# Nine conditioning steps spread through the first half's second merge, and residual tiles for the last recurrent block in the second half alone

## The chip, the cores and the metric

One core of a Trainium2 chip runs the kernel. The metric is the device time of one execution in microseconds; several executions are timed and their median stands. TensorE is called PE here, VectorE DVE, ScalarE ACT, GpSimd POOL and SyncE SP.

## The reference

One decoder layer for a prompt of 1024 tokens and for 8 samples of 4 tokens, which share the weights. Model width is 1024.

```python
mod = silu(c) @ ada_w + ada_b                       # conditioning: 6 x 1024 values per sequence
sh1, sc1, gt1, sh2, sc2, gt2 = split(mod, 6)
h = rmsnorm(x, norm1_g) * (1 + sc1) + sh1
u_x, u_g, u_q, u_k, u_v, u_r, u_lr, u_ga, u_gb = split(h @ w_in)
xc = causal_conv(u_x)
y_a = rg_lru(xc) * gelu(u_g)                        # 10 recurrent blocks of 128 channels
y_b = norm(gla_chunked(u_q, u_k, u_v, u_lr)) * silu(u_r)
m = sigmoid(u_ga) * (y_a @ proj_a) + sigmoid(u_gb) * (y_b @ proj_b)
x = x + gt1 * (m @ w_out)
h2 = rmsnorm(x, norm2_g) * (1 + sc2) + sh2
f1, f2 = split(h2 @ ffn_w1)
x = x + gt2 * ((silu(f1) * f2) @ ffn_w2)
```

The outputs are the two activations and the states of the convolution, of the recurrence and of the chunked branch.

## The kernel before

The tokens are worked in two halves: A has 512 columns of the prompt, B the other 512 and the 32 of the samples. Activations stand with channels in partitions. A weight is loaded in f32 (tiles `raw`, a ring of 5), and split into a high and a low part of a narrower type (tiles `hl`, a ring of 3; ACT writes the high part at line 154, DVE the low one at 155). A product then takes three matrix multiplications per 128 input channels: high by high, high by low and low by high (lines 452, 453, 454).

**The merge.** For each of eight blocks j of 128 output channels, a first loop makes the gate `gbpsa` (24 matrix multiplications) and the product `pbpsa` with `proj_b` (24, from eight tiles `yba`), and keeps their combination `mba` (line 1207). That loop is woven with the recurrent blocks. Then a second loop, `merge_a`, makes for each j the gate `gapsa` (24) and the product `papsa` with `proj_a`: 15 matrix multiplications with the weight tile `pa0` and the recurrent outputs `yaa0` to `yaa4`, and 15 with `pa1` and `yaa5` to `yaa9`.

**The conditioning steps.** `ada_w` is 48 quarters of 512 KB, named ada00 to ada113 (chunk 0 to 11, quarter 0 to 3). The last eight chunks belong to the generator `ada_rest`: each step multiplies one quarter (line 212) and loads the next one, only one ahead; it puts the load into a buffer of the S ring (17 buffers, shared with many activations), from SP's queue at line 203. After four quarters a chunk is turned: ACT copies it (line 217), PE transposes it four times (line 223), DVE puts it into `mod` (225, 226, 260). `s.ada(n)` takes n steps. Other generators of half A (`values`, `qk`, `r_tiles`, `merge_b`) take most of them, and nine are left behind the first merge loop: they are the last quarter and the turn of chunk 10, the four quarters and the turn of chunk 11, and two empty steps.

**What else runs there.** `weight_sums` loads pairs of weight tiles `s1`, `s2` (named `s_raw` in the profile) into the same ring of `raw` tiles, makes sums of them on DVE (lines 352 to 355) and has POOL write them out (357 when 353 is done, 356 when 355 is done). `paced_sums` has POOL copy one column of a gate's tile into a `sums` tile (line 387), so that the load behind it (388) doesn't start earlier than that gate; DVE sums them (392 to 396), and POOL writes (398). A scheduler of the framework orders each engine's instructions by priority and readiness as it estimates them, and `AHEAD` lifts the weights' splits. So an edit in one place can change the order on several engines.

**The recurrent block.** `lru_gate` makes the decay `a` and the state `hh` of a block. Both are in one tile of the S ring, except for the last block, where two tiles of the X ring (8 buffers, which also hold the residuals) are taken: lines 1100 to 1104. The exponential of line 1106 writes `a`; DVE then makes the input (1109, 1122), scans (1129), multiplies with the gelu gate (1138), and the result is split (188, 189) into `yaa`.

Of the kernel before, what the change touches and what calls it, by code (L numbers as in the profile page):

```python
# [18 lines left out]
NR = 10  # L19
# [35 lines left out]
def hybrid_layer(ctx, tc, I, O):  # L55
# [32 lines left out]
    def S(name, dt=F32):  # L88
        return sbig.tile([P, 2 * 544], dt, tag="S", name=name)

    def T(name, w=544):
        return tp.tile([P, w], F32, tag="t", name=name)
# [50 lines left out]
    def load_raw(src, n, name):  # L143
        raw = wp.tile([P, 1024], F32, tag="raw", name=name + "_raw", bufs=5)
        sp.dma_start(raw[:, :n], src)
        return raw
# [169 lines left out]
    def drain(g):  # L316
        for _ in g:
            pass

    def chain(*gs):  # L320
        for g in gs:
            yield from g

    def weave(g, extra, n):
        for w in g:
            yield w + sum(next(extra, 0.0) for _ in range(n))

    def side(g, extra):
        for w in g:
            next(extra, None)  # L330
            yield w
        yield from extra

    def mix(main, fill):
        credit = 0.0
        for want in main:
            credit = min(credit, 3.0) - want
            while credit < 0:
                got = next(fill, None)
                if got is None:  # L340
                    break
                credit += got
# [60 lines left out]
    class Half:  # L403
# [684 lines left out]
        def lru_gate(s, nb, m, xc):  # L1088
            N, n = s.N, f"{s.n}{nb}"
            gw = load_raw(I["lru_w"][nb], 256, "lw" + n)  # L1090
            g1, g2 = s.wide("g1" + n), s.wide("g2" + n)
            for g, c in (g1, 0), (g2, P):
                for o, w, bank, off in [(0, HP, 0, 0)] if s.hf == 0 else s.parts:
                    pe.matmul(g[:, bank, off:off + w], gw[:, c:c + P], xc[:, o:o + w], start=True, stop=True)
            tr, ti = T("tr" + n), T("ti" + n)
            for t, g, b in (tr, g1, nb), (ti, g2, 10 + nb):
                for o, p in s.over(t, g):
                    act.activation(o, p, AF.Tanh, scale=0.5, bias=vh[:, b:b + 1])
            dve.scalar_tensor_tensor(ti[:, :N], ti[:, :N], 1.0, xc[:, :N], op0=OP.add, op1=OP.mult)
            if nb < NR - 1:  # L1100
                both = S("la" + n)
                a, hh = both[:, :N], both[:, 544:544 + N]
            else:
                a, hh = [xp.tile([P, 544], F32, tag="X", name=k + n)[:, :N] for k in ("la", "lh")]
            s4 = sp4[:, nb:nb + 1]
            act.activation(a[:, :N], tr[:, :N], AF.Exp, scale=s4, bias=s4)
            act.activation(tr[:, :N], tr[:, :N], AF.Tanh, scale=s4, bias=s4)
            act.activation(m, a[:, :N], AF.Square)
            dve.scalar_tensor_tensor(m, m, 1.0, tr[:, :N], op0=OP.add, op1=OP.mult)
            return a, hh, ti  # L1110
# [160 lines left out]
        def merge_a(s):  # L1271
            s.m = []
            for j in range(KD):
                tg = s.gate_a(j)
                s.join(j, tg, s.over(tg, s.branch_a(j)))
                s.keep_m(j)
                next(sums_late, None)
                if j % 3 < 2 and j < 7:
                    next(sums_of, None)
# [372 lines left out]
        def branches(s, before):  # L1652
            s.y_a, s.os_ = [None] * NR, []
            b0, b1, v0, v1 = [], [], [], []
            head = chain(s.lr(), s.qk(0, b0))
            if before is not None:
                mix(before, head)
            drain(head)
            g0, g1 = s.values(0, v0), weave(s.values(1, v1), s.adas, 1)
            f = weave(s.qk(1, b1), s.adas, 1)  # L1660
            r = weave(s.r_tiles(), s.adas, 2)
            l = s.lru()
            fill = chain(g0, f, g1, r, l)
            mix(s.gla(0, *b0, g0, v0), fill)
            drain(f)
            mix(side(s.gla(1, *b1, g1, v1), s.head_norm(0)), fill)
            mix(chain(iter([6]), s.head_norm(1)), fill)
            drain(r)
            s.y_b_tiles()
            for w in s.merge_b():  # L1670
                next(l, None)
                next(l, None)
                s.ada(1)
            drain(l)
            drain(s.adas)
            if s.hf:
                pool.dma_start(O["tails"], tails)
            s.merge_a_fast() if s.hf else s.merge_a()
            s.back()
# [137 lines left out]
```

## Time and profile before

| | |
|---|---|
| median of 3 runs | 1961.77 us (1960.86 to 1966.2) |
| profiled execution | 1960.34 us, span 1958.6 us |
| mean granted clock of PE | 0.997 |
| PE busy | 1926.0 us, 13380 matrix multiplications |
| PE's waits on conditioning loads | 6.0 us in 2 waits |

The page gives busy times per engine and the waits with the instruction that ended them. In a timeline, a row has the start and duration in us, the engine and the line, and the tiles written and read; "x8" is a run of eight equal instructions, and a bracket is idle time ahead of the row and what released it. Matrix multiplications overlap, so their pitch is taken from the starts. The sum on the execution starts from 1960.34 us.

### The profile page before, as it was taken

The page shows a single profiled execution, that of the slowest core. Times are in us where ns is not written, and L with a number is a line of the kernel's source. Part 1 is how long each engine was busy: PE and PEld are TensorE (multiplying, and loading weights), DVE is VectorE, ACT ScalarE, POOL GpSimd, SP SyncE. Part 2 cuts the span into 40 slices and gives each one's busy share as a digit, 9 for nine tenths or more (in the row PEclk, how much of TensorE's full clock was granted, in tenths as well). Part 3 has the DMA queues.
Part 4 walks back from the last instruction along what each step waited for, and adds up shares of the span by engine and source line. Part 5 has one row for each costly group of instructions (what it writes and reads, how often), then busy time and mean ns, then how long its engine had stood idle before and what let it go on. Part 6 is the DMA issues. An engine that isn't in the chain of part 4 may idle for free. (4 is left out here: it accounts for less than half of the span.)

```text
span 1958.6 us, 33971 instructions
## 1 busy us (share of the span) xinstructions
PE 1926.0 (98%) x13380; PEld 1753.1 (90%) x13380; DVE 1360.2 (69%) x2420; ACT 973.2 (50%) x1559; POOL 140.7 (7%) x279
## 2 busy tenths in 40 slices
PE   9999999998999999999999999999999999999997
PEld 5877877776899998999899998999999999999997
DVE  5638487774658774677664497786467688888867
ACT  4645375542235552555353366675244354656653
POOL 0000001121100000000000001041201000000000
PEclk9999999999999999999999999999999999999999
DMA  8324235578764357554332413334446534555553
GB/s 341 108 97 165 73 108 193 195 264 315 260 235 157 128 179 247 189 183 156 119 119 68 145 49 96 128 115 148 145 140 226 199 130 131 177 170 179 178 163 104
DMA packets 122240, 319.24 MB, mean 163 GB/s; under 512 B 14560, under 2 KB 29664, under 8 KB 122080
## 3 DMA queue, kind: packets, MB, share of 16 engines
q1 hardware_dynamic: 107536, 263.89, 40.9%
q0 software_dynamic: 14000, 52.62, 7.4%
q8 instruction: 105, 1.72, 0.4%
q10 hardware_dynamic: 544, 0.56, 0.1%
q14 instruction: 55, 0.45, 0.1%
HBM read 278.42 MB, written 38.59 MB: 162 GB/s over the span
## 5 line engine op out<-in xcount | busy, mean ns | idle before, releaser
L155 DVE TENSOR_TENSOR fwa_hl<-fwa,fwa_hl 128x1024 fp32r<-128x1024 f32 (+1 forms) x57 | 68.8, 1207 | 44.6 <-ACT fwa_hl L154 43.6
L155 DVE TENSOR_TENSOR fwb_hl<-fwb,fwb_hl 128x1024 fp32r<-128x1024 f32 (+1 forms) x64 | 77.2, 1207 | 27.7 <-ACT fwb_hl L154 27.7
L154 ACT ACTIVATE fwa_hl<-fwa 128x1024 fp32r<-128x1024 f32 (+1 forms) x57 | 59.3, 1040 | 44.0 <-PE fapsa L1431 10.8
L154 ACT ACTIVATE fwb_hl<-fwb 128x1024 fp32r<-128x1024 f32 (+1 forms) x64 | 66.6, 1041 | 23.4 <-PE fcpsb L1431 9.0
L452 PE MATMUL f3psa<-faa,f3a_hl 128*128 128x512 f32 x176 | 68.6, 390 | 0.6 <-ACT f3a_hl L154 0.6
L454 PE MATMUL f3psa<-faa,f3a_hl 128*128 128x512 f32 x176 | 68.5, 390 | 0.4 <-DVE f3a_hl L155 0.4
L453 PE MATMUL f3psa<-faa,f3a_hl 128*128 128x512 f32 x176 | 68.6, 390 | 0.0
L154 ACT ACTIVATE f3a_hl<-f3a_raw 128x768 fp32r<-128x768 f32 (+1 forms) x32 | 25.4, 792 | 55.7 <-PE f3psa L454 47.4
L155 DVE TENSOR_TENSOR f3a_hl<-f3a_raw,f3a_hl 128x768 fp32r<-128x768 f32 (+1 forms) x32 | 28.3, 888 | 17.4 <-ACT f3a_hl L154 17.0
L452 PEld LDWEIGHTS f3psa<-faa,f3a_hl 128*128 128x128 f32 x176 | 33.0, 188 | 7.7 <-ACT f3a_hl L154 1.0
L454 PEld LDWEIGHTS f3psa<-faa,f3a_hl 128*128 128x128 f32 x176 | 33.0, 188 | 7.6 <-DVE f3a_hl L155 0.9
L453 PEld LDWEIGHTS f3psa<-faa,f3a_hl 128*128 128x128 f32 x176 | 33.0, 188 | 6.8
L352 DVE TENSOR_TENSOR s_raw<-s_raw 128x512 f32<-128x512 f32 x16 | 11.1, 691 | 37.9 <-DMA s_raw<-in_ffn 37.8
L454 PE MATMUL wopsb<-mb,wob_hl 128*128 128x272 f32 x128 | 36.9, 288 | 0.0
L452 PE MATMUL wopsb<-mb,wob_hl 128*128 128x272 f32 x128 | 36.9, 289 | 0.0
L453 PE MATMUL wopsb<-mb,wob_hl 128*128 128x272 f32 x128 | 36.8, 288 | 0.0
L453 PE MATMUL wopsa<-ma,woa_hl 128*128 128x256 f32 x128 | 36.4, 284 | 0.0
L454 PE MATMUL wopsa<-ma,woa_hl 128*128 128x256 f32 x128 | 36.2, 283 | 0.0
L452 PE MATMUL wopsa<-ma,woa_hl 128*128 128x256 f32 x128 | 36.1, 284 | 0.0
L212 PE MATMUL adaps<-ada,cth 128*32 128x256 f32 x384 | 29.5, 397 | 6.2 <-DMA ada<-in_ada_w 6.0
L452 PE MATMUL uxpsa<-h1a,uxpsa_hl 128*128 128x512 f32 x80 | 32.3, 403 | 0.0
L155 DVE TENSOR_TENSOR fvb_hl<-fvb,fvb_hl 128x768 fp32r<-128x768 f32 x28 | 26.8, 956 | 7.7 <-ACT fvb_hl L154 7.4
(2404 smaller groups left out, 7944.9 us busy)
## 6 DMA issues: line engine op xcount, KB each, us to landing
ada<-in_ada_w SPq DMA_DIRECT2D x48, 512.0 KB, 7.9
fwb<-wsum SPq DMA_DIRECT2D x72, 256.0 KB, 3.4
s_raw<-in_ffn SPq DMA_DIRECT2D x32, 512.0 KB, 4.3
wsum<-s_raw POOLq DMA_DIRECT2D x32, 512.0 KB, 4.2
fwa<-wsum SPq DMA_DIRECT2D x64, 256.0 KB, 3.3
fwb<-in_ffn SPq DMA_DIRECT2D x54, 256.0 KB, 3.4
fwa<-in_ffn SPq DMA_DIRECT2D x48, 256.0 KB, 3.1
woa_raw<-in_w_out SPq DMA_DIRECT2D x13, 512.0 KB, 4.2
```

The source lines that it names most:

```text
L154: act.activation(hl[:, 0, :n], raw[:, :n], AF.Copy)
L155: dve.tensor_sub(hl[:, 1, :n], raw[:, :n], hl[:, 0, :n].bitcast(F32))
L212: pe.matmul(ps[32 * g:32 * g + 32, c:c + 256], cth[:, 4 * (k % 2) + g, :], raw[:, g * 256:(g + 1) * 256], start=(k % 2 == 0), stop=(k % 2 ...
L352: dve.tensor_add(r2[:, 512:1024], r2[:, 0:512], r2[:, 512:1024])
L452: pe.matmul(out, wh, x[:, o:o + w], start=st, stop=False)
L453: pe.matmul(out, wh, x[:, N + o:N + o + w], start=False, stop=False)
L454: pe.matmul(out, wl, x[:, o:o + w], start=False, stop=en)
```

## The change

In `merge_a` of half A, each of the eight blocks now takes two conditioning steps, one between gate and product and one behind the product's combination. The `drain(s.adas)` between the two merge loops is gone. The last recurrent block's `a` and `hh` come from an S tile in half A, as for the other blocks, and from two X tiles in half B only.

```diff
@@ -1097,7 +1097,7 @@
-            if nb < NR - 1:
+            if s.hf == 0 or nb < NR - 1:
                 both = S("la" + n)
                 a, hh = both[:, :N], both[:, 544:544 + N]
             else:
@@ -1272,8 +1272,10 @@
             for j in range(KD):
                 tg = s.gate_a(j)
+                s.ada(1)
                 s.join(j, tg, s.over(tg, s.branch_a(j)))
                 s.keep_m(j)
+                s.ada(1)
                 next(sums_late, None)
@@ -1672,7 +1674,6 @@
                 s.ada(1)
             drain(l)
-            drain(s.adas)
             if s.hf:
                 pool.dma_start(O["tails"], tails)
             s.merge_a_fast() if s.hf else s.merge_a()
```

On every engine the order changes between the end of the first merge loop and the second loop of half A; ahead of and behind that it is the same.

**SP's queue** at the loads for the second merge loop. The numbers behind a name are tile numbers; `gapsa`, `pa0`, `pa1` are weights of the merge, `s1`, `s2` the pairs for the sums, `ada` the quarters. Before, ada100 stands ahead of these rows:

```order
L145 DMA pa1a0_raw_3794<-in_proj_a 128x640
L145 DMA s113_raw_3825<-in_ffn1 128x1024
L145 DMA s213_raw_3827<-in_ffn1 128x1024
L145 DMA gapsa1_raw_3836<-in_w_in 128x1024
L203 DMA ada101_3566<-in_ada_w 128x1024
L203 DMA ada102_3626<-in_ada_w 128x1024
L203 DMA ada103_3686<-in_ada_w 128x1024
L203 DMA ada110_3692<-in_ada_w 128x1024
L203 DMA ada111_3709<-in_ada_w 128x1024
L203 DMA ada112_3715<-in_ada_w 128x1024
L203 DMA ada113_3721<-in_ada_w 128x1024
L145 DMA pa0a1_raw_3868<-in_proj_a 128x640
```

And now:

```order
L145 DMA pa1a0_raw_3750<-in_proj_a 128x640
L145 DMA s113_raw_3781<-in_ffn1 128x1024
L145 DMA s213_raw_3783<-in_ffn1 128x1024
L145 DMA gapsa1_raw_3792<-in_w_in 128x1024
L203 DMA ada100_3344<-in_ada_w 128x1024
L145 DMA pa0a1_raw_3834<-in_proj_a 128x640
L145 DMA pa1a1_raw_3854<-in_proj_a 128x640
L145 DMA s114_raw_3892<-in_ffn1 128x1024
L203 DMA ada101_3565<-in_ada_w 128x1024
L203 DMA ada102_3625<-in_ada_w 128x1024
L203 DMA ada103_3685<-in_ada_w 128x1024
L203 DMA ada110_3723<-in_ada_w 128x1024
```

ada100 has moved behind `gapsa1` (it stood three rows ahead of `pa1a0`), ada101 to ada110 behind s114, which waits for POOL's write of s113. ada111 and ada112 come after s115 and s215, and ada113 after s116 and s216.

**DVE** from the sums of s113 to the first product's last tiles. Before, the recurrent blocks 8 and 9 stand well ahead of s113, just before the sums of the pair s111 and s211:

```order
L1109 SCALAR_TENSOR_TENSOR lma8_3310<-lma8_3310,tra8_3317 128x512
L396 TENSOR_TENSOR sums10_3468<-sums10_3468 128x256
L1109 SCALAR_TENSOR_TENSOR lma8_3310<-lma8_3310,tra9_3333 128x512
L1122 TENSOR_TENSOR tia8_3318<-tia8_3318,lma8_3310 128x512
L1122 TENSOR_TENSOR tia9_3334<-tia9_3334,lma8_3310 128x512
L1129 SCALAR_TENSOR_TENSOR laa8_3322<-laa8_3322,tia8_3318 128x512
L352 TENSOR_TENSOR s211_raw_3606<-s211_raw_3606 128x512
```

And now, behind the sums of s113:

```order
L355 TENSOR_TENSOR s113_raw_3781<-s113_raw_3781 128x512
L1207 SCALAR_TENSOR_TENSOR mba6_3601<-gba6_3380,pbpsa6_3571 128x512
L155 TENSOR_TENSOR pa0a0_hl_3732<-pa0a0_raw_3730,pa0a0_hl_3732 128x640
L1109 SCALAR_TENSOR_TENSOR lma8_3310<-lma8_3310,tra9_3333 128x512
L392 TENSOR_TENSOR sums31_3674<-sums31_3674 128x256
L1207 SCALAR_TENSOR_TENSOR mba7_3661<-gba7_3562,pbpsa7_3631 128x512
L1122 TENSOR_TENSOR tia8_3318<-tia8_3318,lma8_3310 128x512
L1122 TENSOR_TENSOR tia9_3334<-tia9_3334,lma8_3310 128x512
L1129 SCALAR_TENSOR_TENSOR laa8_3322<-laa8_3322,tia8_3318 128x512
L1129 SCALAR_TENSOR_TENSOR laa9_3338<-laa9_3338,tia9_3334 128x512
L1138 SCALAR_TENSOR_TENSOR gga8_3412<-laa8_3322,gga8_3412 128x256 x2
L1138 SCALAR_TENSOR_TENSOR gga9_3509<-laa9_3338,gga9_3509 128x256 x2
```

The recurrences of both blocks now stand behind L392 of `sums31` and `mba7`, and ahead of the split of `pa1a0` and of `yaa8`, `yaa9`, which come next. One exponential of line 1106 also has a new wait: for the buffer of `yba0`, which is free when block 7's third matrix multiplication is done.

**PE** at the end of the first merge loop. Before:

```order
L452 MATMUL pbpsa7_3632<-yba7_2243,pba7_hl_3635 128x512
L212 MATMUL adaps10_3565<-ada101_3566,cth_141 32x256 x4
L453 MATMUL pbpsa7_3632<-yba7_2243,pba7_hl_3635 128x512
L454 MATMUL pbpsa7_3632<-yba7_2243,pba7_hl_3635 128x512
L452 MATMUL gapsa0_3741<-h1a0_333,gapsa0_hl_3744 128x512
L453 MATMUL gapsa0_3741<-h1a0_333,gapsa0_hl_3744 128x512
L212 MATMUL adaps10_3565<-ada102_3626,cth_141 32x256 x4
```

And in the first product of `merge_a` now (ada100 stands where ada101 stood above):

```order
L453 MATMUL papsa0_3729<-yaa3_2586,pa0a0_hl_3732 128x512
L212 MATMUL adaps10_3564<-ada101_3565,cth_141 32x256 x4
L454 MATMUL papsa0_3729<-yaa3_2586,pa0a0_hl_3732 128x512
L452 MATMUL papsa0_3729<-yaa4_2790,pa0a0_hl_3732 128x512
L453 MATMUL papsa0_3729<-yaa4_2790,pa0a0_hl_3732 128x512
L454 MATMUL papsa0_3729<-yaa4_2790,pa0a0_hl_3732 128x512
L452 MATMUL papsa0_3729<-yaa5_2916,pa1a0_hl_3752 128x512
L212 MATMUL adaps10_3564<-ada102_3625,cth_141 32x256 x4
```

ada100 has moved from the end of gate 7 (ahead of block 6's product) to there; ada103 comes behind `yaa6`, ada110 ahead of `gapsa2`, ada111 behind the third matrix multiplication of `papsa2`, ada112 ahead of `gapsa3`, ada113 behind the third of `papsa3`.

## Prediction

> **What bounds the kernel now.** I read the page's head first, then the waits of PE, then PE's timeline and the windows around the longest wait, and last the queues that feed it.
>
> ```profile
> span 1958.6 us, 33971 instructions
> PE 1926.0 (98%) x13380; PEld 1753.1 (90%) x13380; DVE 1360.2 (69%) x2420; ACT 973.2 (50%) x1559; POOL 140.7 (7%) x279
> PE adaps L212 <- DMA ada<-in_ada_w: 6.0, 2, 5.6
> ```
>
> PE is busy for 98% of the span: it is the bound, and any time it stands still or runs slowly is on the path. Its largest wait (total, times, longest) is for a load of conditioning weights, 5.6 us at one place. That place is where the change works. PE's timeline there (start, us, instruction, and idle time ahead of it in brackets):
>
> ```profile
> 431.31 0.60 PE L223 MATMUL adat<-ident,accadar 128*128 128x128 f32 x4
> 431.66 0.48 PE L452 MATMUL gbpsa<-h1a,gbpsa_hl 128*128 128x512 f32 x1
> ...
> 436.99 0.39 PE L454 MATMUL gbpsa<-h1a,gbpsa_hl 128*128 128x512 f32 x1
> 437.39 0.64 PE L212 MATMUL adaps<-ada,cth 128*32 128x256 f32 x8
> ...
> 442.87 0.39 PE L452 MATMUL pbpsa<-yba,pba_hl 128*128 128x512 f32 x1
> ...
> 448.31 0.39 PE L452 MATMUL pbpsa<-yba,pba_hl 128*128 128x512 f32 x1
> 454.28 1.08 PE L212 MATMUL adaps<-ada,cth 128*32 128x256 f32 x8 [5.58 <-DMA ada<-in_ada_w]
> ...
> 459.49 0.39 PE L452 MATMUL gapsa<-h1a,gapsa_hl 128*128 128x512 f32 x1
> 459.81 0.64 PE L212 MATMUL adaps<-ada,cth 128*32 128x256 f32 x8
> 460.71 0.39 PE L454 MATMUL gapsa<-h1a,gapsa_hl 128*128 128x512 f32 x1
> ...
> 475.22 0.39 PE L452 MATMUL gapsa<-h1a,gapsa_hl 128*128 128x512 f32 x1
> ```
>
> The two rows at 442.87 and 448.31 are the 22nd matrix multiplication of the merge's blocks 6 and 7, 24 apart: 5.44/24 = 0.227 us each at full clock. From 459.49 to 460.71 lie one conditioning step and two of these (the second stands between the rows shown): 1.22 - 0.45 = 0.77 us for the step. The transposes cost 431.66 - 431.31 = 0.35. From 448.54 (448.31 + 0.227) to 475.22 PE does 56 matrix multiplications (2 of block 7, 24 of the gate, 30 of the product), 7 conditioning steps and 2 transposes: 12.7 + 5.4 + 0.7 = 18.8 us of work. It takes 26.7, so **7.8 us are lost**: 5.58 as the wait, some 2.2 behind it. The windows tell what the 2.2 are (columns: us; busy us of PE, PEld, DVE, ACT, POOL; PE's granted clock, DMA share, GB/s):
>
> ```profile
> 436.00:448.00 12.00, 11.99 (x59) 9.30 (x58) 6.80 (x13) 3.96 (x6) 3.43 (x7) 1.00 0.91 286
> 454.00:459.00 5.00, 4.72 (x22) 2.20 (x23) 4.96 (x10) 0.74 (x1) 1.99 (x4) 0.53 1.02 411
> ```
>
> The granted clock is 0.53 for the five us behind the wait. So the step behind the wait takes 1.08 us, the same step at 459.81 takes 0.64. Another wait of PE, of 2.37 us, leaves no such trace: the matmuls behind it take 0.70 and 0.62.
>
> ```profile
> 1180.13 0.70 PE L1094 MATMUL g1b1l<-xcb,lwb_raw 128*128 128x272 f32 x2 [2.37 <-issue]
> 1180.66 0.62 PE L1094 MATMUL g1b1r<-xcb,lwb_raw 128*128 128x272 f32 x2
> ```
>
> [...]
>
> **Why the load is late** is seen on SP's queue (start, issue time).
>
> ```profile
> 429.02 0.33 SPq L203 DMA_DIRECT2D ada<-in_ada_w  x1
> 444.27 1.24 SPq L145 DMA_DIRECT2D s_raw<-in_ffn  x2
> 446.03 9.72 SPq L203 DMA_DIRECT2D ada<-in_ada_w  x7
> ```
>
> The seven loads are issued together from 446.03, behind two loads for the weight sums; PE wanted the first at 448.5.
>
> **The change part by part.** It adds and removes no arithmetic: the eight loads, eight steps and two turns are the same ones, later. So the sum is the 7.8 given back less the waits in the new places. The residual tiles cost nothing by themselves: no wait in this stretch is for an X tile. Their effect, with that of the order, is that the last recurrent block's la/lh takes a tile of the S ring that the merge's y_b tiles fill, so its exponential waits for block 7's third matrix multiplication, and DVE does that recurrence later. The first product's last tiles need it; I count it in (2).
>
> (1) The step that stood at 437.39 (load ada100) now stands behind 46 matrix multiplications: 437.22 + 46 x 0.227 = 447.7. Its load takes the buffer that block 7's 6th matrix multiplication frees, 437.22 + 30 x 0.227 + 0.4 = 444.4. A load's time to landing is bounded by these answers on DMA issues (KB each, median us; the first has minimum, median, maximum of all 48):
>
> ```profile
> DMA to landing us min/median/max: 3.5/7.9/13.6
> ada<-in_ada_w SPq DMA_DIRECT2D x1, 512.0 KB, 8.2
> s_raw<-in_ffn SPq DMA_DIRECT2D x2, 512.0 KB, 6.3
> s_raw<-in_ffn SPq DMA_DIRECT2D x2, 512.0 KB, 3.2
> ```
>
> At 8.2 the wait is 4.9; at 3.5, 0.2. I take 4.5, near the short end since only the first product's loads share the queue: **1.2 us**.
>
> (2) Next is ada101, in the middle of the first product. PE arrives at 448.9 + 0.77 + 37 x 0.227 = 458.1. The load stands on SP behind s114, which needs the buffer of s113, which is written out by POOL after four DVE operations; PE's progress has no part in it. So everything counts from T, the landing of s113 and s213:
>
> ```profile
> 424.65 0.68 DVE L354 TENSOR_TENSOR s_raw<-s_raw 128x512 f32<-128x512 f32 x1
> 427.58 0.68 DVE L355 TENSOR_TENSOR s_raw<-s_raw 128x512 f32<-128x512 f32 x1
> 451.73 0.69 DVE L352 TENSOR_TENSOR s_raw<-s_raw 128x512 f32<-128x512 f32 x1 [6.89 <-DMA s_raw<-in_ffn]
> 454.34 0.68 DVE L355 TENSOR_TENSOR s_raw<-s_raw 128x512 f32<-128x512 f32 x1
> wsum<-s_raw POOLq DMA_DIRECT2D x2, 512.0 KB, 8.0
> wsum<-s_raw POOLq DMA_DIRECT2D x2, 512.0 KB, 3.8
> ```
>
> Before, T is 451.7. In the new order L355 of an earlier pair (s111) follows L354 at once, 427.58 - 425.25 = 2.3 earlier, and the 512 KB of ada100 are no longer ahead (0.52 MB at 286 GB/s = 1.8): the pair is issued at 444.27 - 4.1 = 440.2. With 6.3 to land, **T = 446.5** (443.4 with 3.2; 451.7 if nothing moves). Then four DVE operations (454.34 - 451.73), the write, s114's issue and ada101's: T + 2.6 + 5.3 + 0.8 + 5.5 = 460.7, with the write between 3.8 and 8.0 and the load between 3.5 and 8.2. **Wait 2.6** (0 to 13.2). Close to the 2.37 case, so I let the clock stand.
>
> DVE has a chain of its own: POOL's second `sums` load waits through gate 7 for the merge's block 6, and DVE's L392 on it stands ahead of the recurrence and the product's split.
>
> ```profile
> 440.10 1.45 POOL L388 DMA_DIRECT2D sums<-in_ffn  x2 [0.18 <-POOL sums L387]
> sums<-in_ffn POOLq DMA_DIRECT2D x2, 256.0 KB, 5.7
> 416.28 1.30 DVE L1122 TENSOR_TENSOR tia<-tia,lma 128x512 f32<-128x512 f32 x2 [2.16 <-ACT lma L1155]
> 417.49 1.22 DVE L1129 TENSOR_TENSOR_SCAN laa<-laa,tia 128x512 f32<-128x512 f32 x1
> 428.19 0.75 DVE L1138 SCALAR_TENSOR_TENSOR gga<-laa,gga 128x256 f32<-128x256 f32 x2
> 454.94 0.68 DVE L1207 SCALAR_TENSOR_TENSOR mba<-gba,pbpsa 128x512 f32<-128x512 f32 x1
> 458.14 0.82 DVE L155 TENSOR_TENSOR pa1a_hl<-pa1a_raw,pa1a_hl 128x640 fp32r<-128x640 f32 x1
> ```
>
> That load goes out at T + 4.9 (2.6 as above, 0.6 for mba, 0.6 for ACT's tanh, 1.1 for POOL), lands 5.1 later (a little under 5.7), and DVE then needs 0.35 (half of an L352) + 0.6 + 1.25 + 2 x 1.2 + 2 x 0.75 + 0.75 = 6.8: T + 16.8 = 463.3. PE, held by ada101, reaches that split's low half at 460.7 + 2 steps + 6 matrix multiplications = 463.6. Nothing more is lost; if the load came early, this chain would still cost 463.3 - 461.0 = 2.3, so a fast load alone would change (2) little.
>
> (3) ada111 and ada113 go out behind loads that the split of a product's second tile releases, about 2.3 us after that product's end; PE needs them 24 + 3 matrix multiplications and a step later, 6.9. That leaves 4.6; at 5.4 to landing (between 3.2 and 6.3) **0.8 each**, 0 to 3.6 (at 8.2).
>
> Sum: 1.2 + 2.6 + 1.6 = 5.4 against 7.8: 2.4 us gained, 1960.34 - 2.4 = 1957.9 on the profiled execution's basis. The median shown, 1961.77, is 1.4 above that execution, so 1959.4 is my figure.
>
> [...]
>
> **The rivals.** *All is hidden.* Loads land in 3.5 and T is 443.4: ada101 lands by 458, DVE's chain ends before PE comes at 461.0, the waits come to about 1, and 6.8 are gained: 1955.0. Against it: T needs every step early, and the DMA engines' share is 0.91 to 1.02 in the windows shown. Chance 0.12.
>
> *Transfers stay as slow as before* (the side that is slower). T stays 451.7, the write takes 8.0, loads 8.2. ada100 waits 4.9, the clock falls (2.2), PE arrives at 458.1 + 3.7 + 2.2 = 464.0; ada101 lands at 451.7 + 2.6 + 8.0 + 0.8 + 8.2 = 471.3: 7.3 and again 2.2; with (3) 18.2, a loss of 10.4: 1972.2. It decides from where waits and slow clock pass 7.8. For it: the median landing of 7.9. Against: the burst of seven loads is gone. Chance 0.12.
>
> *The later pair is the stall.* ada111 and ada113 at 8.2 wait 3.6 each, and the clock falls twice: 1.2 + 2.6 + 2 x (3.6 + 2.2) = 15.4, a loss of 7.6: 1969.4. Against: no burst of seven loads is in those stretches, and the pair of `s_raw` loads lands in 3.2 to 6.3 in the stretches that they move to. Chance 0.08.
>
> *The wait only moves.* ada100 takes 8.2, the clock falls, what follows is covered by that delay: 4.9 + 2.2 = 7.1 for 7.8: 1961.1. It is the case that the change doesn't do what it says. Chance 0.13.
>
> **How the numbers follow.** Mine has 0.55, with a range of its own from half and double the waits: 1960.34 + 1.4 less 7.8, plus 2.7 or 10.8, 1956.7 to 1964.8. About 0.3% (5.9 us) is what a measurement can tell from no change. Faster by that needs under 1955.9: the first rival, 0.12. Slower needs over 1967.7: the second and third, 0.20. Within: 0.68. The range runs from 1954.5, below the first rival, to 1968, which leaves out the two slow cases.
>
> **What would show it.** In the changed profile: no wait of 5.58 at 448; one under 2 there before adaps; one of about 2.6 inside the first product; clock 1.00 in the windows from 444 to 475; DVE idle ahead of a `sums` operation; waits under 1 in the third and fourth products. A clock near 0.5 in any of these windows, or a wait near the 5.58 of before at one of the steps, would make the prediction wrong to the slow side; a first product without any wait, to the fast side.

## The result, and the profile after

The changed kernel takes 1971.43 us (median of 6 runs, 1968.84 to 1977.0), the kernel before 1962.05 in the same comparison (6 runs, 1959.07 to 1966.2). The ratio is 1.0050 with an interval of 1.0031 to 1.0069: slower by 6 to 13.5 us. The forecast was 2.4 us faster. The profiled execution took 1968.84 us with a span of 1967.0, 8.4 more than before. Two runs among those reported below, one of the kernel before (3833.69 us) and one of the last variant (6343.93 us), took about two and three times as long and are left out of every ratio.

The page's head and the waits of PE in the changed kernel (total, times, longest):

```profile
span 1967.0 us, 33969 instructions
PE 1928.1 (98%) x13380; PEld 1754.7 (89%) x13380; DVE 1360.5 (69%) x2420; ACT 973.1 (49%) x1559; POOL 145.7 (7%) x279
PE adaps L212 <- DMA ada<-in_ada_w: 10.9, 5, 3.6
PE papsa L454 <- DVE pa1a_hl L155: 1.1, 1, 1.1
```

The work is the same; the waits for conditioning loads grew from 6.0 us in two to 10.9 in five. PE's timeline shows four of the five; the fifth, 0.6 us, lies ahead of these rows:

```profile
432.17 0.60 PE L223 MATMUL adat<-ident,accadar 128*128 128x128 f32 x4
...
451.08 0.64 PE L212 MATMUL adaps<-ada,cth 128*32 128x256 f32 x8 [2.41 <-DMA ada<-in_ada_w]
461.71 0.64 PE L212 MATMUL adaps<-ada,cth 128*32 128x256 f32 x8 [1.36 <-DMA ada<-in_ada_w]
465.77 0.50 PE L454 MATMUL papsa<-yaa,pa1a_hl 128*128 128x512 f32 x1 [1.05 <-DVE pa1a_hl L155]
492.36 0.64 PE L212 MATMUL adaps<-ada,cth 128*32 128x256 f32 x8 [2.89 <-DMA ada<-in_ada_w]
509.92 1.08 PE L212 MATMUL adaps<-ada,cth 128*32 128x256 f32 x8 [3.62 <-DMA ada<-in_ada_w]
...
515.25 0.39 PE L453 MATMUL papsa<-yaa,pa0a_hl 128*128 128x512 f32 x1
...
531.86 0.39 PE L452 MATMUL gapsa<-h1a,gapsa_hl 128*128 128x512 f32 x1
```

The windows around the late waits (us; busy us of PE, PEld, DVE, ACT, POOL; granted clock, DMA share, GB/s):

```profile
444.00:475.00 31.00, 26.18 (x133) 19.02 (x132) 20.55 (x33) 12.59 (x17) 10.68 (x12) 1.00 0.79 282
482.00:493.00 11.00, 8.11 (x47) 5.51 (x45) 6.47 (x11) 2.91 (x4) 1.15 (x3) 1.00 0.90 312
510.00:515.00 5.00, 5.00 (x18) 3.36 (x19) 2.68 (x4) 0.60 (x1) 1.09 (x2) 0.50 0.65 229
```

The wait of 5.58 us at 448 and its slow clock (0.53 from 454 to 459) are gone. In their place stand three small waits with a full clock, and then two that were not there: 2.89 us for ada111, and 3.62 us for ada113 with the clock at 0.50 behind it. From 509.92 to 515.25 PE does one step and ten matrix multiplications, 0.77 + 2.27 = 3.0 us of work, in 5.33: 2.3 us of slow clock.

Both kernels do the same work between two landmarks that the change leaves alone: the transposes that stand at 431.31 before and at 432.17 now, and the first matrix multiplication of the gate of block 5, which stands here in the profile of before:

```profile
524.40 0.39 PE L452 MATMUL gapsa<-h1a,gapsa_hl 128*128 128x512 f32 x1
```

That is 93.1 us before and 531.86 - 432.17 = 99.7 now: **the stretch lost 6.6 us**. I call this stretch the second merge below. The sum of the new waits and the slow clock, 2.41 + 1.36 + 1.05 + 2.89 + 3.62 + 2.3 = 13.6, less the 7.8 of before, gives 5.8 of them; 0.8 stay that these rows do not place. The rest of the 8.4 lies outside, where the orders are the same: 0.9 ahead of the first landmark (432.17 - 431.31) and 0.9 behind the second. What lies behind is slow clock in the second half: 0.66 from 1187 to 1192 now, and 1.00 from 1180 to 1185 in the profile of before. From the second landmark to the wait at 1180.13 in the profile of before, which the prediction shows, both kernels take nearly the same time (655.7 us before, 655.3 now); from there to the end it is 778.5 and 779.8. The wait is the same, and yet the instructions behind it are slower now than the 0.70 and 0.62 us of before:

```profile
1187.18 0.91 PE L1094 MATMUL g1b1l<-xcb,lwb_raw 128*128 128x272 f32 x2 [2.38 <-issue]
1187.88 1.11 PE L1094 MATMUL g1b1r<-xcb,lwb_raw 128*128 128x272 f32 x2
```

### The profile page after: what moved, and what is told of

Read it like the earlier page. It is cut to its first block, busy times and chain, and to the rows that moved or that the text cites. A ratio compares the mean times of both kernels' runs of the same rounds, so it can differ in the third digit from the quotient of the medians.

```text
span 1967.0 us, 33969 instructions
## 1 busy us (share of the span) xinstructions
PE 1928.1 (98%) x13380; PEld 1754.7 (89%) x13380; DVE 1360.5 (69%) x2420; ACT 973.1 (49%) x1559; POOL 145.7 (7%) x279
## 5 line engine op out<-in xcount | busy, mean ns | idle before, releaser
L212 PE MATMUL adaps<-ada,cth 128*32 128x256 f32 x384 | 29.5, 393 | 11.3 <-DMA ada<-in_ada_w 10.9
L212 PEld LDWEIGHTS adaps<-ada,cth 128*32 128x32 f32 x384 | 9.2, 109 | 27.4 <-DMA ada<-in_ada_w 12.2
```

Source lines behind the costliest of these rows:

```text
L212: pe.matmul(ps[32 * g:32 * g + 32, c:c + 256], cth[:, 4 * (k % 2) + g, :], raw[:, g * 256:(g + 1) * 256], start=(k % 2 == 0), stop=(k % 2 ...
```

## The experiments

Every kernel was compared with the kernel before on the same chip, whose median in these comparisons lies between 1960.81 and 1962.17 us; the ratios are therefore a better guide than the medians. The "stretch" column is the second merge's length in one profile less the 93.1 us of before. Second profiles of three kernels, at the end, differ by 0.6 to 1.8 us in it. In the two late starts the turn of chunk 11 stands behind the second landmark, so its 0.35 us is added there.

| kernel | median us | ratio to before (interval) | stretch, us |
|---|---|---|---|
| changed | 1971.43 | 1.0050 (1.0031 to 1.0069) | +6.6 |
| spread alone | 1967.20 | 1.0038 (1.0025 to 1.0052) | +5.8 |
| tiles alone | 1965.94 | 1.0030 (1.0018 to 1.0041) | +2.3 |
| changed, loads two ahead | 1962.56 | 1.0004 (0.9993 to 1.0014) | -0.1 |
| changed, ACT's queue | 1970.73 | 1.0055 (1.0040 to 1.0071) | +6.3 |
| spread alone, loads two ahead | 1963.55 | 1.0007 (0.9996 to 1.0019) | -0.2 |
| changed, pairs elsewhere | 1967.86 | 1.0029 (1.0015 to 1.0044) | -2.8 (see there) |
| tiles alone, no late sums | 1959.45 | 0.9990 (0.9981 to 1.0000) | -4.5 |
| late start | 1959.41 | 0.9989 (0.9979 to 0.9999) | -1.7 |
| late start, three ahead | 1959.01 | 0.9987 (0.9976 to 0.9997) | -7.3 |

### One half of the change at a time

The spread alone leaves the tile choice of before:

```diff
-            if s.hf == 0 or nb < NR - 1:
+            if nb < NR - 1:
```

> The steps are spread through the second merge as in the change; the last block keeps its two residual tiles. Theory (the spread alone makes the two late waits, the tiles alone remove the early one): the early wait of 5.6 us on the conditioning load near 448 stays with its slow clock, 7.8 us; to it come waits of about 2.9 us in the third product and 3.6 us in the fourth with some 2.2 us of slow clock behind it: 8.7 us slower than before, about 1970.7 us, slower by 0.44%. Rival (the late waits come from the S ring that the la/lh tile shortens, so only both edits together make them): no late wait, 1962 us, within 0.3% of before.

PE's timeline of the spread alone:

```profile
453.60 1.08 PE L212 MATMUL adaps<-ada,cth 128*32 128x256 f32 x8 [4.39 <-DMA ada<-in_ada_w]
...
508.42 1.08 PE L212 MATMUL adaps<-ada,cth 128*32 128x256 f32 x8 [3.91 <-DMA ada<-in_ada_w]
```

The early wait stays (4.39, with the step behind it at 1.08, the slow clock). Of the late ones only that for ada113 came in this profile, and ada111's step had none. The loss is 5.8 us in the stretch and 6.4 by the medians; the ratio's interval, 4.9 to 10.2 us, takes in the 8.7 expected. The sign and the place are the theory's for ada113: the spread alone makes that late wait and keeps the early one. Why ada111 did not wait here comes below.

The tiles alone put the other line into the kernel of before:

```diff
-            if nb < NR - 1:
+            if s.hf == 0 or nb < NR - 1:
```

> The last recurrent block takes one S tile in the first half; all steps stay right behind the first merge loop. Theory: the early waits are those of the change (2.4, 1.4 and 1.1 us, full clock) in place of 7.8 us, and there is no late wait: 3 us faster than before, about 1959 us, within 0.3%. Rival (seven loads in one burst behind s114 saturate the queues): the wait inside the first product grows to 4 us or more with a slow clock, 1963 us or more.

```profile
449.27 0.64 PE L212 MATMUL adaps<-ada,cth 128*32 128x256 f32 x8 [1.60 <-DMA ada<-in_ada_w]
460.37 0.64 PE L212 MATMUL adaps<-ada,cth 128*32 128x256 f32 x8 [1.85 <-DMA ada<-in_ada_w]
466.83 0.80 PE L454 MATMUL papsa<-yaa,pa1a_hl 128*128 128x512 f32 x1 [3.47 <-DVE pa1a_hl L155]
466.00:472.00 6.00, 5.17 (x18) 3.03 (x19) 3.08 (x5) 2.90 (x4) 3.66 (x3) 0.51 0.46 136
```

This is not the gain of 3 us that I expected. The two waits for loads are small, but the wait for the second split of the first product (pa1) is 3.47 us, and the clock falls to 0.51 behind it. The late thing is neither a load nor PE, but the chain on DVE. The rows of DVE in this kernel:

```profile
458.37 0.43 DVE L392 TENSOR_TENSOR sums<-sums 128x256 f32<-128x256 f32 x1 [5.53 <-DMA sums<-in_ffn]
465.95 0.82 DVE L155 TENSOR_TENSOR pa1a_hl<-pa1a_raw,pa1a_hl 128x640 fp32r<-128x640 f32 x1
```

DVE stands 5.53 us before L392, then needs 7.6 to the split. So the tile edit by itself removes the early wait and pays for it with the DVE chain. The profiled execution is 8.4 us longer than that of before; the stretch holds 2.3 of them, and the rest is in the second half (see the second profile, at the end).

The chain's cause was tried by taking the sum away from that place:

```diff
-                if s.hf or j >= 4:
+                if s.hf or 4 <= j < 7:
                     next(sums_late, None)
                     next(sums_late, None)
```

> The tiles alone, and POOL's paced sums make no step at the first merge's last block, so that no sum waits on DVE ahead of the last recurrences. Theory (the wait for the first product's second split comes from the sums load that holds DVE): that wait of 3.5 us with its slow clock is gone, the waits of 1.6 and 1.9 us on ada100 and ada101 stay: some 5 us less than with the tiles alone, about 1960.5 us. Rival (the recurrence is late because its S tile comes late): a wait of 2 us or more on that split or on the recurrent outputs stays, 1964 us or more.

The wait at the split is gone, and the ratio to before falls from 1.0030 with the tiles alone to 0.9990, as expected. In place of the two waits for loads that were expected there is one, 2.98 us for ada100, and the clock stays at 1.00 from 440 to 475:

```profile
450.94 0.64 PE L212 MATMUL adaps<-ada,cth 128*32 128x256 f32 x8 [2.98 <-DMA ada<-in_ada_w]
...
440.00:475.00 35.00, 32.02 (x182) 21.76 (x181) 22.54 (x39) 15.00 (x20) 4.83 (x9) 1.00 0.86 323
1550.85 0.39 PE L454 MATMUL wopsb<-mb,wob_hl 128*128 128x272 f32 x1 [2.68 <-DVE wob_hl L155]
```

The theory holds: `sums` ahead of the recurrence on DVE made it. This profile is the slowest of the kernel's 11 runs (1964.8 us). It loses its gain in the second half, in part by a wait of 2.68 us that no other profile has; that the sums made later cause it was not shown.

### Why the late loads are late

Loads two ahead from ada110 on, in the changed kernel:

```diff
             n = 4 * cc + k + 1
-            if n < 48:
-                ada_next.append(ada_load(n // 4, n % 4))
+            for n in (n, n + 1) if n == 42 else (n + 1,) if n > 42 else (n,):
+                if n < 48:
+                    ada_next.append(ada_load(n // 4, n % 4))
```

> The changed kernel, but from ada110 on the loads run two quarters ahead of their steps, so ada111 goes out with ada110 and ada113 with ada112. Theory (the late waits are those of loads that stand at the end of a burst of SP loads and are wanted 7 us after it): no wait over 0.5 us in the third and fourth products, 8.7 us less than the changed kernel, about 1962 on the measure of the changed kernel's 1971 and 1959.5 by its early waits: within 0.3% of before. Rival (the engines are saturated, the transfers late wherever they are issued): waits of 2 us or more stay in those products or come to splits of the product's weights, 1968 us or more.

No step behind ada102 waits, and the time is 1962.56, 8.9 us under the changed kernel's: the late pair's price is near what the two waits and the slow clock add up to, 2.89 + 3.62 + 2.3 = 8.8. The stretch differs by 6.7 only, since in this profile the clock fell to 0.66 from 450 to 455, behind a wait of 2.18 us for ada100. One wait of 1.0 us came up at a gate's split. The same edit with the spread alone:

> The spread alone with the residual tiles as before, and from ada110 on the loads run two quarters ahead. Theory: the early wait of 4.4 to 5.6 us near 448 stays with its slow clock, the late waits are gone: as before, 1961 us. Rival (the late waits move to other loads): 1965 us or more.

It gives 1963.55, stretch -0.2: the early wait of 4.25 us is there, and the late ones are not.

When the loads go out, and how long they take, in the changed kernel (SP's issues; then the DMA issues in windows of about 1 us around them: KB each, median us to landing):

```profile
482.53 0.54 SPq L145 DMA_DIRECT2D pa0a_raw<-in_proj_a  x1
483.29 0.33 SPq L145 DMA_DIRECT2D pa1a_raw<-in_proj_a  x1
483.72 0.87 SPq L145 DMA_DIRECT2D s_raw<-in_ffn  x2
484.64 0.90 SPq L203 DMA_DIRECT2D ada<-in_ada_w  x2
...
501.73 0.42 SPq L203 DMA_DIRECT2D ada<-in_ada_w  x1
...
ada<-in_ada_w SPq DMA_DIRECT2D x2, 512.0 KB, 8.5
...
ada<-in_ada_w SPq DMA_DIRECT2D x1, 512.0 KB, 8.1
```

The row with 8.5 is for ada111 and ada112, issued together; ada111 by itself lands in 7.7. They go out behind four loads of 1664 KB in sum that were issued within 2.1 us. ada113 goes out behind four of the same sizes within 2.5 us, while POOL issues two loads of 384 KB. The engines are full meanwhile: from 486 to 492 their share is 0.99, all of it (99.0%) SP's queue and none of it POOL's, so POOL's writes do not hold up ada111. Is it the place in SP's queue, or what the engines have to move? ACT was given the last three loads:

```diff
-        sp.dma_start(raw[:, :1024], I["ada_w"][cc, k])
+        (act if 4 * cc + k in (45, 46, 47) else sp).dma_start(raw[:, :1024], I["ada_w"][cc, k])
```

> The changed kernel, but ada111, ada112 and ada113 are issued by ACT, behind its copies for the combination, which is at about the same time (some 0.5 us later) as SP issued them. If they were late because SP's queue serves what was issued ahead of them first, they now land in 4 to 5.5 us: waits under 1 us, 1962 to 1964 us. If all transfers share the engines whoever issues them, the landing stays at 7.5 to 8 us or comes later: waits of 2.9 and 3.6 us with a slow clock, or more, 1970 us.

```profile
ada<-in_ada_w ACTq DMA_DIRECT2D x2, 512.0 KB, 7.5
...
ada<-in_ada_w ACTq DMA_DIRECT2D x1, 512.0 KB, 8.2
...
488.87 0.64 PE L212 MATMUL adaps<-ada,cth 128*32 128x256 f32 x8 [2.58 <-DMA ada<-in_ada_w]
508.47 1.08 PE L212 MATMUL adaps<-ada,cth 128*32 128x256 f32 x8 [4.08 <-DMA ada<-in_ada_w]
```

From ACT's queue they land in 7.5 and 8.2 us, against 8.5 and 8.1 from SP's, the waits are about the same (2.58 and 4.08 for 2.89 and 3.62), and so is the time (1970.73). So it is not the place in SP's queue.

If it is the bytes in flight, taking the pair `s115`, `s215` away from ada111 must help ada111 alone:

```diff
-                if j % 3 < 2 and j < 7:
+                if j in (0, 4, 5, 6, 7):
                     next(sums_of, None)
```

> The changed kernel with the pairs of loads for the weight sums at other blocks of the second merge, so that no such pair stands ahead of ada111, while one (s114, s214) stands ahead of ada113. Theory (a late load is late by the bytes that are in flight at its issue, above all the 1 MB of the pair): ada111 lands within 6 us, its wait is under 1 us; ada113 waits about 3 us as in the changed kernel. Rival (POOL's writes and sums or the issue time make it late): both waits stay near 3 us.

```profile
482.04 0.86 SPq L203 DMA_DIRECT2D ada<-in_ada_w  x2
ada<-in_ada_w SPq DMA_DIRECT2D x2, 512.0 KB, 4.7
...
502.09 0.64 PE L212 MATMUL adaps<-ada,cth 128*32 128x256 f32 x8 [1.43 <-DMA ada<-in_ada_w]
554.24 0.79 PE L454 MATMUL gapsa<-h1a,gapsa_hl 128*128 128x512 f32 x1 [6.01 <-DVE gapsa_hl L155]
```

ada111 and ada112 land in 4.7 us (the median of the two) and their steps do not wait; ada113, still behind a pair, lands in 6.2 and waits 1.43 (less than the 3 I expected). The edit moved more than the pair, though: the gate's weight and `pa1` went out at other times as well, and `pa0`, 320 KB, is the only load in the 3.8 us ahead of ada111. And a pair ahead is not enough. In the spread alone, where ada111 did not wait, the pair stands right ahead of it too, but its two loads are issued over 3.73 us and `pa1` 3 us before them:

```profile
482.07 3.73 SPq L145 DMA_DIRECT2D s_raw<-in_ffn  x2
485.85 0.90 SPq L203 DMA_DIRECT2D ada<-in_ada_w  x2
ada<-in_ada_w SPq DMA_DIRECT2D x2, 512.0 KB, 4.8
```

So a late landing goes here with the bytes issued close ahead (8.5 us for the two behind 1664 KB within 2.1 us, 4.7 behind 320 KB in 3.8 us), and not with the pair as such (4.8 behind a pair issued over 3.73 us). That is read from these rows; no run changed the spacing alone. The kernel gains nothing by the moved pairs, as a gate's split waits 6.01 us at the end of the merge, where the pairs now stand; that they make this wait was not tried. The table's stretch ends ahead of it.

### A better place for the steps

Starting from the spread with the residual tiles of before and the loads two ahead, the last iterations of the first merge loop take no step. The step on ada101, the one that waited 5.58 us, moves to the end of the first gate:

```diff
-            for w in s.merge_b():
+            for i, w in enumerate(s.merge_b()):
                 next(l, None)
                 next(l, None)
-                s.ada(1)
+                if i < 13:
+                    s.ada(1)
```

> The steps are spread through the second merge with the residual tiles as before, the last iterations of the first merge loop take no step (so the step on ada101 moves 26 matrix multiplications back, 5.9 us, to the end of the first gate), and from ada110 on the loads run two quarters ahead. Theory (a load is hidden when it is issued some 9 us ahead of its step and goes out at a place where few others do): no wait over 0.5 us on a conditioning load, full clock between 444 and 530, the 7.8 us are gained: about 1953 us, 0.4% faster than before. Rival (the DMA engines are full in this stretch, so the wait only moves to another load or to a split of a weight): waits of 3 us or more in sum come up there, 1958 us or more, no measurable change.

```profile
PE papsa L455 <- DVE pa0a_hl L155: 1.6, 2, 0.8
PE adaps L212 <- DMA ada<-in_ada_w: 1.3, 2, 1.0
PE gapsa L455 <- DVE gapsa_hl L155: 0.7, 1, 0.7
...
500.00:520.00 20.00, 18.28 (x83) 13.49 (x82) 10.57 (x16) 4.88 (x7) 2.18 (x4) 0.91 0.88 326
```

The early wait is gone, but 3.6 us of small waits are left, and the clock is at 0.91 from 500 to 520: 1.7 gained in the stretch. The rival was right: the waits moved, to splits above all, they sum to more than the 3 us it named, and the time is over its 1958. What was left stood mostly at ada112, issued behind a pair. Its load, and with it that of ada113, was moved ahead by one more step:

```diff
-            for n in (n, n + 1) if n == 42 else (n + 1,) if n > 42 else (n,):
+            for n in (n, n + 1) if n == 42 else (n + 1, n + 2) if n == 44 else (n + 2,) if n > 44 else (n + 1,) if n > 42 else (n,):
```

> The late start, with the load of ada112 moved ahead by one more step, so that it goes out with ada110 and ada111 and only ada113 stands behind the pair s116, s216. Theory (what the late start still loses after 500 is ada112 behind that pair): its wait of 1.0 us and the 0.7 us at the gate's split behind it are gone with the slow clock there, some 3.5 us less than the late start: 1956 us, 0.3% faster than before. Rival (the stretch is full, the wait goes to the next load): no change, 1959.5 us.

```profile
PE gapsa L455 <- DVE gapsa_hl L155: 0.2, 1, 0.2
...
440.00:475.00 35.00, 35.00 (x170) 27.23 (x169) 18.53 (x27) 9.90 (x14) 6.75 (x12) 1.00 0.91 332
475.00:515.00 40.00, 39.78 (x196) 30.29 (x195) 22.90 (x37) 11.46 (x16) 6.70 (x12) 1.00 0.82 298
```

In the profile 7.3 of the 7.8 us are gained: PE stands still for 0.2 us from 440 to 515. That execution took 1954.69 us. The median of its runs is 1959.01, though, and the ratio 0.9987 (0.9976 to 0.9997): faster than before, but by 0.6 to 5 us, and hardly faster than the version ahead of it. So the theory holds for this stretch, and the time is the rival's. Its runs lie between 1954.69 with a granted clock of 0.998 and 1962.63 with 0.996. Where the slower ones lose that is not in this profile, and stays open.

### The same kernels once more

Three kernels ran again for a second profile.

> The changed kernel once more, for a second profile. Its runs lie between 1968.8 and 1977.0 us with granted clocks of 0.995 to 0.991. Theory (how much a wait of some 3 us costs differs by execution: the clock falls behind it or not): the waits are the same within 0.5 us each, and windows behind a wait of 2.4 to 4 us show a clock of 1.00 in one profile and about 0.5 in the other at least at one of the same places. Rival (the transfers differ by execution): the clock falls behind the same waits, and the waits themselves differ by over 1 us.

It took 1966.89 us, with the stretch at +4.8: ada100 waits 1.05, ada101 1.70, ada111 1.87, ada113 3.61. So the places hold, but the waits differ by over 1 us between the two executions, 2.41 and 1.05 for ada100 and 2.89 and 1.87 for ada111, as the rival had it. The clock falls behind ada113 both times, to 0.50 from 510 to 515 and to 0.58 in the window of 505 to 512. Behind ada101 it falls in one profile alone, to 0.68 from 460 to 465, and there the wait is only 1.70 (PE's timeline):

```profile
460.28 0.64 PE L212 MATMUL adaps<-ada,cth 128*32 128x256 f32 x8 [1.70 <-DMA ada<-in_ada_w]
460.85 0.50 PE L454 MATMUL papsa<-yaa,pa0a_hl 128*128 128x512 f32 x1
...
462.54 1.08 PE L212 MATMUL adaps<-ada,cth 128*32 128x256 f32 x8
```

> The kernel before once more, for a second profile. Theory: the early wait is 4.4 to 5.6 us with a slow clock; in the second half, near 1181 and 1260 us, where the first profile kept its full clock, the clock may fall behind the 2.4 us wait and cost 1 to 4 us, as it did in most profiles of the variants. Rival (the second half differs because the changed kernels reach it later): full clock there again.

It took 1960.42 us, with an early wait of 4.38 and a slow step behind it, 0.6 us less in the stretch than in the first profile, and a full clock at 1180 again (the row behind the wait takes 0.70 us), as the rival has it. Lateness is not what decides, though: the spread alone with loads two ahead comes to the same wait at 1180.43, the kernel before at 1180.13 and 1180.34, and only the first has a slow clock behind it (0.66 from 1180 to 1185).

> The tiles alone once more, for a second profile: the first one lost 2 us up to 619 us and 6 us in the second half, its runs are 5 us slower by the median. Theory: the waits on ada100, ada101 and the second split sum to 5 to 8 us again, with a slow clock behind the longest, and the second half's loss differs. Rival: the second half loses the same 6 us again, as a lasting effect of the edit.

It took 1962.99 us, with waits of 2.44, 0.23 and 3.23 and the stretch at +1.7. The second half is 5.3 us shorter than in the first profile of the very same kernel. One place where it shows is the window of 1259 to 1269 us, in the first profile and in the second; the granted clock is the third number from the end:

```profile
1259.00:1269.00 10.00, 9.24 (x41) 7.96 (x40) 7.50 (x24) 7.61 (x15) 0.34 (x2) 0.66 0.40 133
```

```profile
1259.00:1269.00 10.00, 9.50 (x72) 9.11 (x72) 7.99 (x27) 8.47 (x18) 0.34 (x2) 1.00 0.31 96
```

So most of the second half's loss of 6 us in the first profile of this kernel belongs to the execution and not to the edit.

## Why the prediction was wrong, by its own steps

**The bound and the loss to win back** were right. PE sets the time, busy for 98% of the span in both kernels, and the 5.58 us and their slow clock vanished. When nearly all waits are removed (late start, three ahead) the stretch gives 7.3 us, against the 7.8 worked out.

**Step (1)**, ada100, was forecast at 1.2 us and measured 2.41 (1.05 in the second profile), inside its bounds of 0.2 to 4.9.

**Step (2)**, ada101 and the DVE chain, was forecast at 2.6 and measured 1.36 + 1.05 = 2.41. That it came so close is partly luck: the pair that everything counts from landed at 448.5, 2.0 us later than forecast, and PE came to the step 2.2 us later too. The floor that the chain sets was in it: L392 is waited for, the recurrences follow, the split is late. With the tiles alone it was the larger thing, 3.47 us and the slow clock, which I had not seen.

**Step (3)**, ada111 and ada113, is the term that was mis-sized and the step that failed: "0.8 each", measured 2.89 and 3.62, and 2.3 of slow clock behind the second, for which the sum had nothing: 8.8 for 1.6. The times of issue and of need were as worked out: ada111 goes out at 484.64, some 2.3 us behind the product's end, with 4.8 to go to its step. The term that fell is the 5.4 us to landing. It was taken from pairs of `s_raw` loads that landed in 3.2 and 6.3 us, while each of these loads goes out behind such a pair and two weights: ada111 lands in 7.7 and ada113 in 8.1. With less issued close ahead ada111 by itself lands in 3.8 (pairs elsewhere) and 4.3 (the spread alone), and does not wait. My own upper bound was 8.2, so the value was taken from the wrong end: the row nearest in time and not the row nearest in what else is in flight.

With 8.8 for 1.6 my sum gives 5.4 + 7.2 = 12.6 for 7.8: 4.8 slower, 1966.6, on the side that was measured and another 4.8 short of 1971.43. Of these, 1.0 are steps (1) and (2), 0.8 are not placed in the stretch, 0.9 lie ahead of it and 0.9 behind it, and 1.2 come from the basis: I put the median 1.4 above the profiled execution, and here it is 2.6 above. The mechanism is that of the third rival, "the later pair is the stall", to which I gave 0.08 and 1969.4 us. I argued against it that no burst of seven loads is in those stretches. Four loads close together, with the pair among them, were enough: 1664 KB within 2.1 us ahead of ada111, which landed in 7.7.

**"The residual tiles cost nothing by themselves"** was wrong as it stood: the tiles alone make the kernel slower by 0.18 to 0.41%. The order that they give puts 2.3 and 1.7 us of this into the stretch; the rest is not placed.

**The clock.** Step (2) let the clock stand behind a wait near 2.37 us, by one row. That came out in the first profile and not in the second, so it was luck: behind the same wait, 2.37 or 2.38 us at the same instruction of the second half, the next row takes 0.70 us in both profiles of the kernel before, 0.91 and 1.24 in the two of the changed kernel, and 1.25 in the second of the tiles alone and in the late start, three ahead. The third rival let the clock fall behind waits of 3.6 us: an estimate, since the rows had a full clock behind 2.37 and a slow one behind 5.58 and none between. The profile has a fall to 0.50 behind 3.62 and a clock of 1.00 behind 2.89.

**What stays open.** The profiles put 6.6 and 4.8 us into the stretch; the median difference is 9.4, with an interval from 6. Slow clock in the second half is part of the rest in the first profile, some 1.3 us. The changed kernel's runs go from 1968.84 us at a mean clock of 0.995 to 1977.0 at 0.991; 0.004 of the 1928 us of PE's work is 7.7 us, so slow clock would be nearly all of the 8.2 between them, by estimate. Where it lies in the longer runs no profile shows.

## What to carry to other kernels

Price a load by what is in flight when it goes out, not by the nearest load of its size: find the place in the queue, add up the bytes issued in the last two or three us, and take the landing time of a row in such company: here ada111 landed in 7.7 us behind 1664 KB issued within 2.1 us, and in 3.8 behind 320 KB in 3.8 us. Spreading small steps over a loop does not hide their loads by itself (the spread alone lost 5.8 us in the stretch, with waits of 4.39 and 3.91); a load that is issued one step ahead sits where the order puts it, so look for the step with the least time between issue and need. And a tile that changes its ring can move the loads and the chains of other engines more than the instructions that use it (the tiles alone: 3.47 us at the split of `pa1`, behind DVE's L392).

## What the runs showed of the hardware that was not expected

Another queue gave the late loads no advantage: 7.5 and 8.2 us from ACT's queue, 8.5 and 8.1 from SP's, at the same places.

Whether the clock of PE falls is not settled by the length of the last wait alone. It stayed at 1.00 behind waits of 2.41, 2.89 and 2.98 us. It fell behind one of 1.70 (0.68 from 460 to 465, the second profile of the changed kernel) and one of 2.18 (0.66 from 450 to 455, loads two ahead), and behind those of 3.47 (0.51), 3.62 (0.50) and 5.58 us (0.53); behind 3.91, 4.08 and 4.39 us the step took 1.08 us in place of 0.64. The clearest case is the wait of 2.37 or 2.38 us at one instruction of the second half, the same in both kernels: behind it the row took 0.70 us in both profiles of the kernel before, with the clock at 1.00 in the first, and 0.91 and 1.24 in the two of the changed kernel, with the clock at 0.66 in the first. In the late start no single wait passed 1.0 us, and yet the clock is 0.91 from 500 to 520. So a wait of 1.70 us was followed by a slow clock and one of 2.98 was not; what decides it no run showed.
